# A decoder layer on one core: six of eight pairs of gate tiles computed with seven block products instead of eight

## The chip, the core and the metric

The kernel runs on one core of a Trainium2 chip. The metric is the time of one execution in device microseconds. Engines are named as the profile names them: PE is TensorE (PEld its weight loads), DVE is VectorE, ACT is ScalarE, POOL is GpSimd, SP is SyncE, which here only issues DMAs. Each engine works through its own list of instructions in the order in which the program gave them, and a semaphore holds it where it needs another engine's result.

## The reference, cut to what matters

One layer of a decoder for 512 prompt tokens and 64 sample tokens (576 in all), model width 1024. Around the change it computes

```python
z = jnp.einsum('btd,dn->btn', x, w_in)                     # conv B, C, h | q, k, v | two gates of 1024 columns
...
gates = jax.nn.sigmoid(z[..., -2 * D_MODEL:] + b_gate)
mixed = gates[..., :D_MODEL] * (yc @ w_conv_out) + gates[..., D_MODEL:] * (ya @ w_attn_out)
x1 = layer_norm(ALPHA * x + mixed @ w_o, ln1_g, ln1_b)
hid = jnp.square(jax.nn.relu(x1 @ w_up))
x2 = layer_norm(ALPHA * x1 + hid @ w_down, ln2_g, ln2_b)
```

with `yc` the output of a short convolution and `ya` that of attention over three head groups. All of it is float32.

## The kernel before, in words

**Products.** Every float32 operand of a large product is split into a rounded part (hi, an fp32r copy made by ACT) and the rest (lo, source minus hi, made by DVE). A product is then three passes on PE: hi by hi, hi by lo, lo by hi (`PASSES`). Activations stand transposed, features on the 128 partitions, and the 576 tokens are two blocks of 288 columns, so that one matmul is a 128x128 weight against 128x288.

**Weights.** All weights are cut into 126 units of 128x1024 (four bytes each, 512 KB). A `Stream` loads them by SP into a ring of four buffers (`raw`), and splits them into a ring of five (`hl`). `get(u)` gives unit u and writes the splits of the next ones into the lists of ACT and DVE at that place. The order of all work is written out by hand: what the Python code emits first stands first in an engine's list.

**Stages.** Queries and keys; values; the convolution with attention's softmax and values put between; then the gates, which the change touches; the output projection `o` (line 1028); the first norm; and the feed-forward part in four quarters, up (`up_pair`) and down.

**The gates (lines 953 to 981).** For each j of 8 there are two gate tiles (units u and u+1, 48 matmuls each, named `zg`), and one unit of 768 columns that holds `w_conv_out` and `w_attn_out` for the same 128 features (36 matmuls, named `zm`: 24 for the convolution, 12 for attention). ACT makes the sigmoids from PSUM (line 964), DVE multiplies the two `zm` tiles by them (line 973) and adds (976), and ACT and DVE split the sum into `mxhl` (lines 542 and 543), which the output projection reads. A `zg` or `zm` tile takes two PSUM banks and there are two such tiles; of the other four banks two are used as `s` and two as `ya0` and `ya1` in the stages before, and lie idle in the gates.

**Seven products (`up_pair`, line 1166).** The up part of the feed-forward uses already what the change brings to the gates. Two weight tiles A and B of 1024 inputs against two blocks of tokens are a product of 2 by 2 blocks (A1, A2 and B1, B2 are the halves over the inputs): eight block products of 12 matmuls each. A Strassen-Winograd scheme does it with seven, of sums of weight blocks and sums of x blocks. The weights come as four pieces: `hu` (unit A as it is), `hs` and `hc` (two tiles of sums), and `hd` (half of unit B). `raws` holds the sums: SP loads B2 and A1 into it, POOL issues a DMA that adds B1 to both (`accum_op`, line 327), and DVE adds A1 and A2 later (lines 367 and 369). The sums of x are made by DVE, and split as everything is. PE then makes seven products into three banks (`a`, `Y`, `X`). After the first product ACT copies bank `a` away (`p1`, line 1178), the third product adds on in `a`, and DVE makes the outputs from `Y`, `X` and `p1` (lines 1183 to 1204). `Stream.queue`, `load`, `hi`, `lo`, `pump` and `next` (lines 293 to 392) keep that: `hi` writes the next ACT cast of a weight piece if its ring has a free buffer, `lo` the next DVE job behind it.

Of the kernel before, what the change touches and what calls it, by code (L numbers as in the profile page):

```python
# [20 lines left out]
F32 = mybir.dt.float32  # L21
# [219 lines left out]
class Stream:  # L241


    def __init__(self, nc, pool, wall):
        self.nc, self.pool, self.wall = nc, pool, wall
        self.raw, self.hl = {}, {}
        self.loaded = self.done = 2
        self.last = FIRST_F + ALONE - 1
# [41 lines left out]
        return self.hl.pop(u)  # L290


    def queue(self, items, pool, held):
# [15 lines left out]
        self.got = {}

        self.hls.held = [[t, False] for t in held]

    def load(self):
        Q = self.nc.sync
        while self.loads:
            n, it = self.loads[0]
            rings = (self.raws,) if it[0] == "unit" else (self.raws, self.raws2, self.raw1)
            if not all(r.free() for r in rings):
                return
            self.loads.pop(0)  # L320
            one = self.wall[it[1] - 2]
            if it[0] == "pair":
                two = self.wall[it[2] - 2]
                sums = self.raws2.take(f"raws{it[1]}")
                Q.dma_start(sums[:, 0, :], two[:, 512:])
                Q.dma_start(sums[:, 1, :], one[:, :512])
                self.nc.gpsimd.dma_start(sums, two[:, :512].unsqueeze(1).broadcast_to((128, 2, 512)), accum_op=ALU.add)  # L327
            r = self.raws.take(f"raw{it[1]}")
            Q.dma_start(r, one)
            self.got[n] = [r]  # L330
            if it[0] == "pair":
                last = self.raw1.take(f"rawl{it[1]}")
                Q.dma_start(last, two[:, 512:])
                self.got[n] += [sums, last]

    def hi(self):

        self.load()
        if not self.pieces:
            return  # L340
        n, kind, ring = self.pieces[0]
        ring = getattr(self, ring)
        if n not in self.got or ring is None or not ring.free() or (kind == 2 and ("sum", n) in self.after):
# [6 lines left out]
        w = 512 if kind == 3 else 1024  # L350
        t = ring.take(f"h{'uscd'[kind]}{n}")
        self.nc.scalar.copy(t[:, 0, :w], src[:, :w])  # L352
# [81 lines left out]
def _decoder_step(ctx, tc, nc, a):  # L434
# [86 lines left out]
    def last_rows(pool, x, name):  # L521

        t = pool.tile([128, 8, 2, 64], F32R, tag=name, name=name)
        for s in range(2):
            G.tensor_copy(t[:, :, s, :], x[:, s, :, 512:576])
        return t.rearrange("p k s n -> p k (s n)")

    def rows_of(x, last, xs, k, t):
        return x[:, xs, k, 128 * t:128 * t + 128] if t < 4 else last[:, k, :]
# [421 lines left out]


    mx_stack, mxpool = pool("mx", "right")
    mxhl = mxpool.tile([128, 2, 8, NT], F32R, tag="mxhl", name="mxhl")
    gt_stack, gtpool = pool("gt")
    for j in range(8):
        sg = []
        for i in range(2):
            z, zs = z_tile(f"zg{j}{i}")
            f_tile(stream.get(u), xhl, 8, zs)  # L960
            u += 1
            t = gtpool.tile([128, 2, NB], F32, tag=f"sg{i}", name=f"sg{j}{i}")
            c = C_BG + 8 * i + j
            S.activation(t, z, AF.Sigmoid, bias=con[:, c:c + 1], scale=1.0)  # L964
            sg.append(t)
        w = stream.get(u)
        u += 1
        m = []
        for i, (x, nk, w0) in enumerate(((ychl, 4, 0), (yahl, 2, 512))):
            z, zs = z_tile(f"zm{j}{i}")  # L970
            f_tile(w, x, nk, zs, w0)
            t = gtpool.tile([128, 2, NB], F32, tag=f"m{i}", name=f"m{j}{i}")
            V.tensor_tensor(t, z, sg[i], ALU.mult)  # L973
            m.append(t)
        mm = gtpool.tile([128, 2, NB], F32, tag="mm", name=f"mm{j}")
        V.tensor_tensor(mm, m[0], m[1], ALU.add)
# [96 lines left out]
    for i in range(4):  # L1073
        b_tile(f"none{i}")
    outs = [b_tile(f"o0{t}") for t in range(5)]
    for kk in range(4):
        w = stream.get(u)
        u += 1
# [4 lines left out]
    ws = [stream.get(u + kk, 7 - kk) for kk in range(4)]  # L1083
    u += 4
    for t in range(5):
        out = b_tile(f"o1{t}")
        for kk in range(4):
# [63 lines left out]
        return (lambda: S.copy(x1T[:, 0, m], t),  # L1151
                lambda: V.tensor_tensor(x1T[:, 1, m], t, x1T[:, 0, m].bitcast(F32), ALU.subtract))

    def product(z, w, w0, x, start):
        for i in range(4):
            for n, (ws, xs) in enumerate(PASSES):
                T.matmul(z, lhsT=w[:, ws, w0 + 128 * i:w0 + 128 * i + 128], rhs=x(xs, i),  # L1157
                         start=(start and i == 0 and n == 0), stop=(i == 3 and n == 2), skip_group_check=True)
# [7 lines left out]
    def up_pair(q, f, prev):  # L1166

        h = stream.next()
        ha, hb, hc, hd = (h[kind] for kind in range(4))
        z, Y, X = (half_bank(f"{b}{q}{f}") for b in "aYX")  # L1170
        p1 = fp.tile([128, NB], F32, tag="p1", name=f"p1{q}{f}", bufs=2)
        cc = cc_tile(f"cc{q}{f}")
        product(z, ha, 0, part_of(0, 0), True)
        stream.hi()
        prev[0]()
        stream.lo()
        product(Y, hc, 0, sum_of(2), True)
        S.copy(p1, z)
        prev[1]()
        stream.lo()  # L1180
        product(z, ha, 512, part_of(1, 0), False)
        stream.hls.done(ha)
        V.tensor_tensor(cc[:, 2], Y, p1, ALU.add)
        prev[2]()
        stream.lo()
        product(Y, hb, 0, sum_of(0), False)
        S.activation(cc[:, 0], z, AF.Relu)
        prev[3]()
        stream.hi()
        product(X, hb, 512, sum_of(1), True)  # L1190
        stream.hls.done(hb)
        V.tensor_tensor(cc[:, 3], Y, p1, ALU.add)
        stream.lo()
        stream.hi()
        product(Y, hc, 512, part_of(1, 1), False)
        stream.hls.done(hc)
        V.tensor_tensor(cc[:, 3], X, cc[:, 3], ALU.add)
        stream.lo()
        stream.hi()
        product(X, hd, 0, sum_of(3), False)  # L1200
        stream.hl1.done(hd)
        V.tensor_tensor(cc[:, 1], Y, p1, ALU.add)
        stream.lo()
        V.tensor_tensor(cc[:, 2], X, cc[:, 2], ALU.add)
# [206 lines left out]
```

## Time and profile before

| what | value |
|---|---|
| median of 3 runs | 852.58 us (852.41 to 853.11) |
| profiled execution, its own time | 852.76 us, span 850.7 us, clock 0.995 |
| gates, first `zg` to first `o` matmul | 247.51 to 389.32 us |
| one j of the gates | 17.60 us, of it 12.80 `zg` and 4.80 `zm` |
| busy in 250 to 300 us | PE 50.0, DVE 17.1, ACT 14.1, POOL 0 us |
| busy in 450 to 500 us (pairs of up, start of down) | PE 49.8, DVE 39.2, ACT 37.3, POOL 1.6 us |

How to read the views: a row of the timeline has the start, the length, the engine, the line, the operation, output and input tiles, the shape, how many instructions were put together, and in brackets how long the engine was idle before and what ended that. A row of the groups has busy time and mean nanoseconds of one, then the idle time before them. A matmul's length in the trace covers its way through the array, and matmuls overlap: what one costs in a stream is seen from the starts, not from the lengths.

### The profile page before, as it was taken

Reading aid. Unit: us, or ns where it says so; the run is one execution under the profiler, and the core shown is the slowest. Engines: PE = TensorE matmul, PEld = TensorE weight load, DVE = VectorE, ACT = ScalarE, POOL = GpSimd, SP = SyncE. Lnnn points to the kernel's source line nnn. Section 1 sums busy time; section 2 is a strip of 40 time slices with the busy share of each in tenths; the row PEclk is TensorE's granted clock in tenths of the full one; section 3 lists DMA queues with packets and bytes.
Section 4 is the critical chain, followed back from the end, with each engine's and each line's share of the span. In section 5 each row is a group of like instructions: output and inputs, shape, how many; then the busy total and the mean of one; then the engine's idle time right before and its main releaser. Section 6 shows DMA issues by size and latency. Waiting matters only on the chain.

```text
span 850.7 us, 14971 instructions
## 1 busy us (share of the span) xinstructions
PE 832.0 (98%) x6312; PEld 803.2 (94%) x6312; DVE 452.8 (53%) x747; ACT 317.0 (37%) x531; POOL 78.9 (9%) x117
## 2 busy tenths in 40 slices
PE   7999999999999999999999999999999999999994
PEld 7999999898889999998889999999999999999993
DVE  6545555574243344334769753476345753476465
ACT  6111126822223223322359631266114641266231
POOL 0212000137000000001001010000100000000013
PEclk9999999999999999999999999999999999999997
DMA  9687653871212232335207262444635262453111
GB/s 342 221 283 245 217 174 129 301 271 47 67 53 73 83 93 70 93 92 185 83 20 205 73 193 67 115 123 145 152 88 137 75 186 63 112 137 125 50 44 68
DMA packets 37762, 112.68 MB, mean 132 GB/s; under 512 B 4640, under 2 KB 4960, under 8 KB 37536
## 3 DMA queue, kind: packets, MB, share of 16 engines
q1 hardware_dynamic: 33840, 102.30, 36.7%
q0 software_dynamic: 3856, 9.44, 5.6%
q8 instruction: 49, 0.80, 0.4%
q14 instruction: 17, 0.14, 0.0%
HBM read 93.85 MB, written 16.42 MB: 130 GB/s over the span
## 4 chain that ended last, share of the span: by engine, by line
PE 94%; DVE 4%; ACT 1%; DMA 0%; issue 0%; POOL 0%; ACTq 0%
PE d L1126 18%; PE zg L512 12%; PE Y L1157 8%; PE d L1119 6%; PE o L1028 6%; PE a L1157 5%; PE X L1157 5%; PE v L879 5%; PE zA L512 5%; PE zm L512 5%; PE zB L512 4%; PE zh L512 3%; PE zc L512 2%; PE zb L512 2%; PE u L1119 2%; PE ya L720 1%
## 5 line engine op out<-in xcount | busy, mean ns | idle before, releaser
L1126 PE MATMUL d<-hid,hu 128*128 128x288 f32 x1152 | 154.1, 296 | 0.0
L1126 PEld LDWEIGHTS d<-hid,hu 128*128 128x128 f32 x1152 | 153.8, 189 | 0.0
L267 DVE TENSOR_TENSOR hl<-raw,hl 128x1024 fp32r<-128x1024 f32 (+1 forms) x64 | 76.4, 1204 | 102.3 <-ACT hl L266 102.0
L512 PE MATMUL zg<-xhl,hl 128*128 128x288 f32 x768 | 103.7, 296 | 0.0
L512 PEld LDWEIGHTS zg<-xhl,hl 128*128 128x128 f32 x768 | 102.8, 189 | 0.0
L266 ACT CAST hl<-raw 128x1024 fp32r<-128x1024 f32 (+1 forms) x64 | 65.0, 1020 | 67.3 <-PE zA L512 26.6
L352 ACT CAST hu<-raw 128x1024 fp32r<-128x1024 f32 x46 | 47.6, 1049 | 53.3 <-PE d L1126 37.7
L372 DVE TENSOR_TENSOR hu<-raw,hu 128x1024 fp32r<-128x1024 f32 x46 | 55.5, 1217 | 1.2 <-ACT hu L352 1.2
L1119 PE MATMUL d<-hid,hu 128*128 128x320 f32 (+1 forms) x384 | 53.4, 298 | 0.0
L1119 PEld LDWEIGHTS d<-hid,hu 128*128 128x128 f32 x384 | 51.5, 189 | 0.0
L1157 PE MATMUL a<-x1hl,hu 128*128 128x288 f32 x336 | 49.9, 297 | 0.0
L512 PE MATMUL zA<-xhl,hl 128*128 128x288 f32 x288 | 43.1, 304 | 4.5 <-ACT xhl L490 4.5
L1157 PEld LDWEIGHTS a<-x1hl,hu 128*128 128x128 f32 x336 | 46.6, 188 | 0.3
L1028 PE MATMUL o<-hl,mxhl 128*128 128x512 f32 x192 | 45.6, 394 | 0.8 <-DVE m L973 0.8
L512 PEld LDWEIGHTS zA<-xhl,hl 128*128 128x128 f32 x288 | 40.4, 194 | 5.6 <-ACT xhl L490 4.5
L1028 PEld LDWEIGHTS o<-hl,mxhl 128*128 128x128 f32 x192 | 35.8, 188 | 9.0 <-DVE m L973 1.1
L327 POOL DMA_DIRECT2D raws<-in_wall x14 | 16.9, 1207 | 281.2 <-DMA raws<-in_wall 152.5
L1356 DVE TENSOR_TENSOR yT<-yT,d 128x288 f32<-128x288 f32 x32 | 13.1, 451 | 51.7 <-PE d L1126 51.7
L879 PE MATMUL v<-hl,xhl 128*128 128x256 f32 x288 | 37.7, 287 | 0.0
L879 PEld LDWEIGHTS v<-hl,xhl 128*128 128x128 f32 x288 | 35.3, 191 | 2.1 <-issue 1.6
L964 ACT ACTIVATE sg<-zg,con 128x576 f32<-128x576 f32 x16 | 11.9, 741 | 59.2 <-PE zg L512 59.2
L512 PE MATMUL zB<-xhl,hl 128*128 128x288 f32 x240 | 33.5, 297 | 0.0
(202 smaller groups left out, 1308.6 us busy)
## 6 DMA issues: line engine op xcount, KB each, us to landing
raw<-in_wall SPq DMA_DIRECT2D x102, 512.0 KB, 4.7
raws<-in_wall SPq DMA_DIRECT2D x28, 256.0 KB, 4.2
raws<-in_wall POOLq DMA_DIRECT2D x14, 512.0 KB, 8.5
kc<-in_kc SPq DMA_DIRECT2D x8, 512.0 KB, 4.2
out_kc_out<-kc SPq DMA_DIRECT2D x8, 512.0 KB, 6.4
vc<-in_vc SPq DMA_DIRECT2D x8, 512.0 KB, 5.6
out_vc_out<-vc SPq DMA_DIRECT2D x8, 512.0 KB, 8.3
rawl<-in_wall SPq DMA_DIRECT2D x14, 256.0 KB, 4.3
```

What stands on the lines that cost most here:

```text
L266: self.nc.scalar.copy(hl[:, 0, :w], raw[:, :w])
L267: self.nc.vector.tensor_tensor(hl[:, 1, :w], raw[:, :w], hl[:, 0, :w].bitcast(F32), ALU.subtract)
L327: self.nc.gpsimd.dma_start(sums, two[:, :512].unsqueeze(1).broadcast_to((128, 2, 512)), accum_op=ALU.add)
L352: self.nc.scalar.copy(t[:, 0, :w], src[:, :w])
L372: V.tensor_tensor(t[:, 1, :w], src[:, :w], t[:, 0, :w].bitcast(F32), ALU.subtract)
L512: T.matmul(z[blk], lhsT=w[:, ws, w0 + 128 * k:w0 + 128 * k + 128], rhs=x[:, xs, k, NB * blk:NB * blk + NB], start=(k == 0 and n == 0), sto ...
L879: T.matmul(out, lhsT=rows_of(xhl, xlast, xs, k, t), rhs=wk[:, ws, kk:kk + 256], start=(k == 0 and n == 0), stop=(k == 7 and n == len(passe ...
L1028: T.matmul(out, lhsT=rows_of(mxhl, mlast, xs, k, t), rhs=w[:, ws, 512 * i:512 * i + 512], start=(k == 0 and m == 0), stop=(k == 7 and m == ...
L1119: T.matmul(z, lhsT=w[:, ws, 128 * k:128 * k + 128], rhs=x[:, xs, k, FB[blk]], start=(k == 0 and n == 0), stop=(k == 7 and n == 2), skip_gr ...
L1126: T.matmul(z[blk], lhsT=w[:, ws, 128 * k:128 * k + 128], rhs=x[:, xs, k, NB * blk:NB * blk + NB], start=(k == 0 and n == 0), stop=(k == 7 ...
L1157: T.matmul(z, lhsT=w[:, ws, w0 + 128 * i:w0 + 128 * i + 128], rhs=x(xs, i), start=(start and i == 0 and n == 0), stop=(i == 3 and n == 2), ...
L1356: V.tensor_tensor(y, y, z[blk], ALU.add)
```

## The change: what it does

For j = 2 to 7 the two gate tiles are a pair of seven products; j = 0 and 1 stay as they were. The body of `up_pair` becomes a function `pair`, used by the gates and by `up_pair`. In the gates its three banks are the idle `s`, `ya0` and `ya1`.

- `xr`: x is loaded once more, as float32, in two DMAs of 1.15 MB, into the place where the second half of `mxhl` will be. `gate_sum` makes the four sums of its blocks in place (DVE, line 1017 and on, then a cast by ACT, line 1024), `gate_low` the rest (DVE, line 1027). Sums 0 and 1 stand behind the merge of j = 0, sums 2 and 3 behind the two gate tiles of j = 1.
- The units 36 to 58 (six pairs, their `zm` units, and five units of the output projection) come by `queue` rather than by `get`. The sums of a pair are now a load of their own. The order of pieces in the gates is hs, hd, hc, hu.
- `merge` does what lines 968 to 977 did; the sigmoids lie in one tile `cc`, with one buffer, and the products and the sum are written into it.
- `mxhl` becomes two tiles, `mxa` and `mxb`, for j = 0 to 3 and 4 to 7.

```diff
+    def gate_sum(m):
...
+        if m == 0:
+            V.tensor_tensor(b11, b11, b12, ALU.subtract)
...
+        S.copy(xT[:, 0, m], (b11, b12, b22, b21)[m])
+    def gate_low(m):
+        V.tensor_tensor(xT[:, 1, m], (b11, b12, b22, b21)[m], xT[:, 0, m].bitcast(F32), ALU.subtract)
...
     for j in range(8):
-            S.activation(t, z, AF.Sigmoid, bias=con[:, c:c + 1], scale=1.0)
...
-        split_into(mxhl[:, 0, j], mxhl[:, 1, j], flat(mm))
+        cc = gtpool.tile([128, 4, NB], F32, tag="cc", name=f"gc{j}")
+        if j < G_ALONE:
...
+                if j == 0 and i == 0:
+                    Q.dma_start(xr[:, 0:4, :], a["start"][:, 0:4, 256:])
+                    Q.dma_start(xr[:, 4:8, :], a["start"][:, 4:8, 256:])
+                    stream.queue(items, gtpool, [], (1, 3, 2, 0))
...
+                f_tile(w, xhl, 8, zs)
+                u += 1
+                if j:
+                    stream.hls.done(w)
+                    gate_sum((2, 3)[i])
+                S.activation(cc[:, 2 * i:2 * i + 2], z, AF.Sigmoid, bias=bias(i, j), scale=1.0)
+                if j:
+                    gate_low((2, 3)[i])
+                    stream.pump(2)
+            w = stream.get(u)
+            merge(j, w, cc)
...
+        else:
+            p1 = gtpool.tile([128, NB], F32, tag="p1", name=f"gp{j}", bufs=2)
...
+            pair(stream.next(), [t[:, :NB] for t in banks], p1, cc,
...
+            S.activation(cc[:, 1], cc[:, 1], AF.Sigmoid, bias=bias(0, j), scale=1.0)
+            S.activation(cc[:, 2:4], cc[:, 2:4], AF.Sigmoid, bias=bias(1, j), scale=-1.0)
+            w, = stream.next().values()
+            merge(j, w, cc)
+            stream.hls.done(w)
+            stream.pump()
```

The start of `pair`, as it now serves both stages:

```python
        product(z, ha, 0, part_of(0, 0), True)      # product 1 into bank a
        stream.hi()
        prev[0]()
        stream.lo()
        product(Y, hc, 0, sum_of(2), True)          # product 2 into Y
        S.copy(p1, z)
        prev[1]()
        stream.lo()
        product(z, ha, 512, part_of(1, 0), False)   # product 3, adds on in a
        stream.hls.done(ha)
        V.tensor_tensor(cc[:, 2], Y, p1, ALU.add)
        prev[2]()
        stream.lo()
        product(Y, hb, 0, sum_of(0), False)         # product 4, adds on in Y
```

**Where the instructions stand now, first place: ACT between the merge of one j and the next.** Before (ACT, from the merge of j = 1 to the merge of j = 2; `hl39` and on are the splits of weight units, `sg` the sigmoids):

```order
L542 CAST mxhl_2786<-mm1_3112 128x576
L266 CAST hl39_3117<-raw39_2957 128x1024
L964 ACTIVATE sg20_3170<-zg20_3116,con_63 128x576
L266 CAST hl40_3173<-raw40_3013 128x1024
L964 ACTIVATE sg21_3226<-zg21_3172,con_63 128x576
L266 CAST hl41_3228<-raw41_3068 128x768
L542 CAST mxhl_2786<-mm2_3275 128x576
```

With the change (ACT, from the merge of j = 2 to the merge of j = 3; `gp3` is `p1` and `ga3` bank `a` of pair 3, `hs4`, `hd4`, `hc4` and `hu4` the pieces of the pair after, `hu5` the 768 columns of that pair's `zm` unit):

```order
L595 CAST mxa_2792<-gc2_3155 128x576
L359 CAST hs4_3321<-raws42_3138 128x1024
L359 CAST hd4_3341<-rawl42_3144 128x512
L559 COPY gp3_3325<-ga3_3326 128x288
L1092 ACTIVATE gc3_3324<-ga3_3326,con_63 128x288
L359 CAST hc4_3398<-raws42_3138 128x1024
L359 CAST hu4_3418<-raw42_3142 128x1024
L1093 ACTIVATE gc3_3324<-gc3_3324,con_63 128x288
L1094 ACTIVATE gc3_3324<-gc3_3324,con_63 128x576
L359 CAST hu5_3466<-raw44_3153 128x768
L595 CAST mxa_2792<-gc3_3324 128x576
```

The copy of bank `a` stands behind the merge's cast of the j before and behind two casts of weight pieces; before there was nothing between the merge's cast and the next sigmoid but one weight cast.

**Second place: DVE from the merge of j = 0 to the first pair** (`hs0`, `hu0`, `hd0`, `hc0` are the pieces of the pair j = 2):

```order
L596 TENSOR_TENSOR mxa_2792<-gc0_2795,mxa_2792 128x576
L1017 TENSOR_TENSOR xr_2793<-xr_2793 128x4x288
L1019 TENSOR_TENSOR xr_2793<-xr_2793 128x4x288
L1027 TENSOR_TENSOR xT_2794<-xr_2793,xT_2794 128x1152 x2
L1021 SCALAR_TENSOR_TENSOR xr_2793<-xr_2793 128x4x288
L1027 TENSOR_TENSOR xT_2794<-xr_2793,xT_2794 128x1152
L379 TENSOR_TENSOR hs0_3030<-raws36_2802,hs0_3030 128x1024
L374 TENSOR_TENSOR raws36_2802<-raws36_2802,raw36_2962 128x512
L1023 SCALAR_TENSOR_TENSOR xr_2793<-xr_2793 128x4x288
L1027 TENSOR_TENSOR xT_2794<-xr_2793,xT_2794 128x1152
L376 TENSOR_TENSOR raws36_2802<-raws36_2802,raw36_2962 128x512
L379 TENSOR_TENSOR hu0_3033<-raw36_2962,hu0_3033 128x1024
```

Behind them come the rest of `hd0`, the product with `zm10`, the rest of `hc0`, and the product with `zm11`. Before, three splits of weight units stood in their place. ACT's list there reads: three casts of sums, the sigmoid of `zg10`, casts of `hs0` and `hu0`, the cast of the fourth sum, the sigmoid of `zg11`, casts of `hd0`, `hc0`, `hu1`, the merge's cast, `hs2`, `hd2`, the copy of bank `a`.

**Third place: DVE behind the merge of j = 2:**

```order
L596 TENSOR_TENSOR mxa_2792<-gc2_3155,mxa_2792 128x576
L379 TENSOR_TENSOR hs4_3321<-raws42_3138,hs4_3321 128x1024
L374 TENSOR_TENSOR raws42_3138<-raws42_3138,raw42_3142 128x512
L376 TENSOR_TENSOR raws42_3138<-raws42_3138,raw42_3142 128x512
L564 TENSOR_TENSOR gc3_3324<-gY3_3327,gp3_3325 128x288
```

The first reading of bank `Y` (line 564) stands behind the merge's split, the split of `hs4` and both sums of weights for the pair after; before, one split of a weight unit stood behind the merge. Pair 7 has only one split of a unit (`hu12`) in the place of the three.

More of the change, by code (lines that the diff above doesn't have):

```diff
@@ L315, in load @@
         while self.loads:
-            n, it = self.loads[0]
-            rings = (self.raws,) if it[0] == "unit" else (self.raws, self.raws2, self.raw1)
-            if not all(r.free() for r in rings):
+            n, it, sums = self.loads[0]
+            rings = (self.raws2,) if sums else (self.raws,) if it[0] == "unit" else (self.raws, self.raw1)
+            if not all(r.free() for r in rings) or (self.sums_only and not sums):
                 return
@@ L342, in hi @@
         ring = getattr(self, ring)
-        if n not in self.got or ring is None or not ring.free() or (kind == 2 and ("sum", n) in self.after):
+        if n not in self.got or self.got[n][0] is None or ring is None or not ring.free() or (kind == 2 and ("sum", n) in self.after):
             return
@@ L523, in last_rows, with product, pair @@
         t = pool.tile([128, 8, 2, 64], F32R, tag=name, name=name)
[L524 to L525 removed]
+        n = 8 // len(x)
+        for i, part in enumerate(x):
+            for s in range(2):
+                G.tensor_copy(t[:, n * i:n * i + n, s, :], part[:, s, :, 512:576])
         return t.rearrange("p k s n -> p k (s n)")
     def rows_of(x, last, xs, k, t):
[L529 removed]
+        n = 8 // len(x)
+        return x[k // n][:, xs, k % n, 128 * t:128 * t + 128] if t < 4 else last[:, k, :]
     def passes_of(t):
         return PASSES if t < 4 else ((0, 0), (0, 1))
+    def product(z, w, w0, x, start):
+        for i in range(4):
+            for n, (ws, xs) in enumerate(PASSES):
+                T.matmul(z, lhsT=w[:, ws, w0 + 128 * i:w0 + 128 * i + 128], rhs=x(xs, i),
+                         start=(start and i == 0 and n == 0), stop=(i == 3 and n == 2), skip_group_check=True)
+    def pair(h, banks, p1, cc, part_of, sum_of, prev, eleven):
+        ha, hb, hc, hd = (h[kind] for kind in range(4))
+        z, Y, X = banks
+        product(z, ha, 0, part_of(0, 0), True)
+        stream.hi()
+        prev[0]()
+        stream.lo()
+        product(Y, hc, 0, sum_of(2), True)
+        S.copy(p1, z)
+        prev[1]()
+        stream.lo()
+        product(z, ha, 512, part_of(1, 0), False)
+        stream.hls.done(ha)
+        V.tensor_tensor(cc[:, 2], Y, p1, ALU.add)
+        prev[2]()
+        stream.lo()
+        product(Y, hb, 0, sum_of(0), False)
+        eleven(cc[:, 0], z)
+        prev[3]()
+        stream.hi()
+        product(X, hb, 512, sum_of(1), True)
+        stream.hls.done(hb)
+        V.tensor_tensor(cc[:, 3], Y, p1, ALU.add)
+        stream.lo()
+        stream.hi()
+        product(Y, hc, 512, part_of(1, 1), False)
+        stream.hls.done(hc)
+        V.tensor_tensor(cc[:, 3], X, cc[:, 3], ALU.add)
+        stream.lo()
+        stream.hi()
+        product(X, hd, 0, sum_of(3), False)
+        stream.hl1.done(hd)
+        V.tensor_tensor(cc[:, 1], Y, p1, ALU.add)
+        stream.lo()
+        V.tensor_tensor(cc[:, 2], X, cc[:, 2], ALU.add)
     def z_tile(name):
@@ L1075, in _decoder_step @@
     outs = [b_tile(f"o0{t}") for t in range(5)]
+    stream.last = FIRST_F + ALONE - 1
+    stream.loaded = stream.done = FIRST_O + 5
     for kk in range(4):
-        w = stream.get(u)
-        u += 1
+        w, = stream.next().values()
         for t in range(5):
@@ L1082, in _decoder_step @@
                 o_add(outs[t], t, 0)
-    ws = [stream.get(u + kk, 7 - kk) for kk in range(4)]
-    u += 4
+        if kk == 0:
+            assert not stream.after or len(stream.pieces) == 0
+        while stream.pieces or stream.after:
+            stream.pump()
+            if kk < 2:
+                break
+        if not stream.pieces and not stream.after and kk < 3:
+            stream.prepare(FIRST_O + 5 + kk, 0)
+    ws = list(stream.next().values()) + [stream.get(FIRST_O + 5 + kk, 6 - kk) for kk in range(3)]
+    u = FIRST_F
     for t in range(5):
@@ L1168, in up_pair @@
         h = stream.next()
-        ha, hb, hc, hd = (h[kind] for kind in range(4))
-        z, Y, X = (half_bank(f"{b}{q}{f}") for b in "aYX")
+        cc = cc_tile(f"cc{q}{f}")
         p1 = fp.tile([128, NB], F32, tag="p1", name=f"p1{q}{f}", bufs=2)
[L1172 to L1204, printed above, removed]
+        pair(h, [half_bank(f"{b}{q}{f}") for b in "aYX"], p1, cc, part_of, sum_of, prev,
+             lambda c, z: S.activation(c, z, AF.Relu))
         def rectify():
```

117 lines of the change are left out of this document (77 added, 40 removed).

## The prediction

> **What bounds the kernel now.** I read the page first, then the timeline of the gates engine by engine, then the groups of instructions for prices, then the pairs of the feed-forward part, where the same scheme runs already.
>
> ```profile
> span 850.7 us, 14971 instructions
> PE 832.0 (98%) x6312; PEld 803.2 (94%) x6312; DVE 452.8 (53%) x747; ACT 317.0 (37%) x531; POOL 78.9 (9%) x117
> PE 94%; DVE 4%; ACT 1%; DMA 0%; issue 0%; POOL 0%; ACTq 0%
> ```
>
> PE is busy for 98% of the span and holds 94% of the chain that ended last. So a matmul less is time less, if PE still never waits. In the gates it does not wait at all (PE, one j):
>
> ```profile
> 282.71 12.96 PE L512 MATMUL zg<-xhl,hl 128*128 128x288 f32 x96
> 295.51 3.36 PE L512 MATMUL zm<-ychl,hl 128*128 128x288 f32 x24
> 298.71 1.76 PE L512 MATMUL zm<-yahl,hl 128*128 128x288 f32 x12
> 300.31 12.96 PE L512 MATMUL zg<-xhl,hl 128*128 128x288 f32 x96
> ```
>
> One j takes 300.31 - 282.71 = 17.60 us for 132 matmuls, 0.1333 us each; 12 of them, a product, take 1.60.
>
> **What is removed.** Six pairs times 12 matmuls: 72 x 0.1333 = 9.60 us. An undisturbed pair with its `zm` would take 16.00. Added: on PE nothing; on ACT and DVE casts, sums and copies. Over a whole j both have room (they are busy 14.1 and 17.1 of 50 us in a stretch of the gates, by the table above). But the order written by hand decides, since PE waits for single instructions in those lists: product 3 for the copy of bank `a`, product 4 for DVE's first reading of `Y`. So I follow both lists from row to row.
>
> **A pair in the middle (j = 3 to 6).** Let t0 be the end of the `zm` before it, where the pair's first product starts. What the merge does after t0 is in the trace, since 282.71 is such a moment (DVE, then ACT, then how the last merge lets go of PE):
>
> ```profile
> 282.91 0.76 DVE L973 TENSOR_TENSOR m<-zm,sg 128x576 f32<-128x576 f32 x1 [0.84 <-PE zm L512]
> 283.70 0.76 DVE L976 TENSOR_TENSOR mm<-m,m 128x576 f32<-128x576 f32 x1
> 285.20 0.76 DVE L543 TENSOR_TENSOR mxhl<-mm,mxhl 128x576 fp32r<-128x576 f32 x1 [0.74 <-ACT mxhl L542]
> 286.15 1.23 DVE L267 TENSOR_TENSOR hl<-raw,hl 128x1024 fp32r<-128x1024 f32 x1 [0.20 <-ACT hl L266]
> ...
> 284.49 0.67 ACT L542 CAST mxhl<-mm 128x576 fp32r<-128x576 f32 x1 [4.86 <-DVE mm L976]
> 285.07 1.05 ACT L266 CAST hl<-raw 128x1024 fp32r<-128x1024 f32 x1
> ...
> 388.51 0.76 DVE L973 TENSOR_TENSOR m<-zm,sg 128x576 f32<-128x576 f32 x1 [0.84 <-PE zm L512]
> ```
>
> ACT's cast for the merge starts at t0 + 1.78 and the cast behind it at t0 + 2.36, 0.09 before the first ends. DVE's next split starts at t0 + 3.44. The new work has its prices in the feed-forward part (groups, with mean ns):
>
> ```profile
> L352 ACT CAST hs<-raws 128x1024 fp32r<-128x1024 f32 x14 | 14.7, 1050 | 37.3 <-PE d L1126 32.1 <-PE X L1157 5.2
> L352 ACT CAST hd<-rawl 128x512 fp32r<-128x512 f32 x14 | 8.6, 618 | 0.0
> L1178 ACT COPY p<-a 128x288 f32<-128x288 f32 x14 | 5.6, 398 | 4.8 <-PE a L1157 4.8
> L372 DVE TENSOR_TENSOR hs<-raws,hs 128x1024 fp32r<-128x1024 f32 x14 | 17.1, 1220 | 2.5 <-ACT hs L352 2.5
> L367 DVE TENSOR_TENSOR raws<-raws,raw 128x512 f32<-128x512 f32 x14 | 9.6, 689 | 0.3
> L1183 DVE TENSOR_TENSOR cc<-Y,p 128x288 f32<-128x288 f32 x14 | 6.4, 456 | 14.6 <-PE Y L1157 14.6
> L1152 DVE TENSOR_TENSOR x1T<-xs,x1T 128x1152 fp32r<-128x1152 f32 x4 | 5.4, 1352 | 0.2 <-ACT x1T L1151 0.2
> L1151 ACT CAST x1T<-xs 128x1152 fp32r<-128x1152 f32 x4 | 4.6, 1152 | 1.4 <-DVE xs L1149 1.4
> ```
>
> *ACT:* `hs` for the next pair from t0 + 2.36, handed over 0.09 before its end: + 0.96; `hd` + 0.53; the copy of `a` from t0 + 3.85 to 4.25. PE goes on 0.05 after a release (the merge's last product ends at 388.51 + 0.76 = 389.27, PE starts at 389.32 below): 4.30. Product 3 would start at t0 + 3.20: **1.10 late**. *DVE:* the split of `hs` from t0 + 3.44, 1.22; two sums of weights, 2 x 0.69; the first reading of `Y`, 0.46: t0 + 6.50, and PE 0.05 later. Product 4 would start at t0 + 4.80: **1.75 late in all** (the 1.10 lie within). The rest of the pair fits: product 7 ends at t0 + 12.95, and all that stands behind on DVE (about 4 us of splits and readings) ends with it. So a middle pair takes 17.75, its own saving of 1.60 and 0.15 more; four of them cost 4 x 1.75 = **7.00**.
>
> In the feed-forward part the same code has no such wait:
>
> ```profile
> 482.64 1.83 PE L1157 MATMUL a<-x1hl,hu 128*128 128x288 f32 x12
> 484.32 1.76 PE L1157 MATMUL Y<-x1T,hc 128*128 128x288 f32 x12
> 485.92 1.76 PE L1157 MATMUL a<-x1hl,hu 128*128 128x288 f32 x12
> 487.52 1.76 PE L1157 MATMUL Y<-x1T,hs 128*128 128x288 f32 x12
> ...
> 484.52 0.40 ACT L1178 COPY p<-a 128x288 f32<-128x288 f32 x1 [0.49 <-PE a L1157]
> ```
>
> There ACT waits for bank `a` (0.49 idle) and copies at once; no merge's cast, which cannot begin before t0 + 1.78, stands ahead of it.
>
> **The last pair (j = 7)** has only one cast ahead of the copy: 2.36 + 0.96 + 0.40 + 0.05 = t0 + 3.77, **0.57** late; DVE is done by 3.44 + 1.22 + 0.46 = 5.12, before product 3 ends at 5.37.
>
> **The first pair (j = 2).** The list of DVE behind the merge of j = 0 is longer than a j. That merge's split starts one j before 285.20, at 267.60, and I let the list go on from 268.3. Sums 0 and 1 (1.36 each, taken as the 1.35 of the splits of their size) end at 271.0, their splits (1.27 each with the handover) at 273.6, sum 2 at 274.9. Its cast on ACT ends at 276.1, its split at 277.5. ACT goes on with a sigmoid, `hs0` and `hu0` to 278.65; DVE splits `hs0` to 278.95, a sum of weights to 279.65, sum 3 to 280.95. Its cast on ACT ends at 282.15; the sigmoid of `zg11` stands behind it and ends at 282.8. The last tile of `zm` needs the banks of `zg11`: it starts at 282.85 instead of 298.71 - 17.60 = 281.11, **1.75 late**. DVE: split of sum 3 to 283.5, a sum 284.2, `hu0` 285.35. Product 1 started at 284.45 and needs that for its third matmul: **0.65**. Then `hd0` 285.95, the product with `zm10` 286.65, `hc0` 287.8; product 2 needs it at 287.0: **0.85**. The product with `zm11` and the addition end at 289.25, then ACT: the merge's cast, `hs2`, `hd2`, the copy, 291.8; product 3 would have started at 289.2: **2.65**. DVE reads `Y` by 293.95 instead of 293.45: **0.55**. Sum **6.45**.
>
> **What a wait costs beside itself.** The first products of `o` come after a wait:
>
> ```profile
> 389.32 5.73 PE L1028 MATMUL o<-hl,mxhl 128*128 128x512 f32 x24 [0.85 <-DVE m L973]
> 395.07 1.20 PE L1028 MATMUL o<-hl,mlast 128*128 128x512 f32 x4
> 396.11 5.63 PE L1028 MATMUL o<-hl,mxhl 128*128 128x512 f32 x24
> 401.58 1.09 PE L1028 MATMUL o<-hl,mlast 128*128 128x512 f32 x4
> ```
>
> 24 matmuls took 5.75 there and 5.47 later: 0.28 for starting again. A wait that a later wait swallows costs none, so six count (the last of each pair). Between 0 and 0.28 I take 0.20: **1.20**.
>
> **The transfers.** x once more, the sums and the pieces lie beside PE:
>
> ```profile
> 239.28 0.34 SPq L947 DMA_DIRECT2D out_ust<-ust  x1
> ...
> 249.21 0.76 DVE L543 TENSOR_TENSOR ychl<-yf,ychl 128x576 fp32r<-128x576 f32 x1 [0.74 <-ACT ychl L542]
> ...
> R<-in_xr SPq DMA_DIRECT2D x1, 2048.0 KB, 9.1
> raws<-in_wall SPq DMA_DIRECT2D x28, 256.0 KB, 4.2
> raws<-in_wall POOLq DMA_DIRECT2D x14, 512.0 KB, 8.5
> ```
>
> SP issues `xr` behind `ust`, near 240; 2.36 MB at the rate of `R` (2048 KB in 9.1) land near 251, 17 us before sum 0. SP then stands until the convolution's tiles are free, near 250; the sums of the first pair have landed (4.2 for the loads, 8.5 for POOL's addition) near 264, needed at 276.7. The sums for pair 4 can be loaded when `hc0` is split (287.8) and land near 302; ACT wants them near 307. So POOL's queue holds nobody up by these rows, with 5 us to spare at its tightest place. Behind the gates nothing changes: `R` and the units behind it wait for the end of the merge as before.
>
> **Sum.** -9.60 + 6.45 + 7.00 + 0.57 + 1.20 = +5.62 us. Against the profiled execution, 852.76 (span 850.7 and 2.06 around it), that is 858.4; the median of the runs, 852.58, lies 0.18 below, so I predict **858.2**. *Bounds.* First pair: DVE without any wait for ACT has 17.3 us of work from 268.3 to `hc0`, so product 2 is 1.0 late at least, and the wait for the copy stays: 4.2; above, with a slower clock (below), 8. Middle pairs: 1.10 each if DVE's reading came in time, 2.20 if both waits added to more: 4.4 to 8.8. Starts: 0 to 1.7. From 852.58 - 0.6 = 852.0 to about 862.
>
> **Rivals.** *The middle pairs run without waits:* then -9.60 + 6.45 + 0.6 for one start again = -2.55, **850.0**, faster. It decides at the copy: if it ends by t0 + 3.2. For it: ACT is busy 28% of the time. Against it: the merge's cast cannot start before t0 + 1.78, and two casts of 1.49 together stand between. 9%. *All of it is hidden*, 852.58 - 9.6 = **843.0**: it needs the first pair's list of 17.3 us in 14.4 as well; 2%. *PE's clock falls in the first pair:* the program's first matmuls, after an idle start, were slow:
>
> ```profile
> 4.48 1.95 PE L512 MATMUL zA<-xhl,hl 128*128 128x288 f32 x6 [4.48 <-ACT xhl L490]
> 6.23 1.65 PE L512 MATMUL zB_first<-xhl,hl 128*128 128x288 f32 x6
> 7.67 1.56 PE L512 MATMUL zA<-xhl,hl 128*128 128x288 f32 x6
> 9.06 0.96 PE L512 MATMUL zB_first<-xhl,hl 128*128 128x288 f32 x6
> ```
>
> 18 matmuls took 9.06 - 4.48 = 4.58 instead of 2.40. If a wait in the gates did that once, 2.2 more: **860.4**. The longest wait that I work out is 2.65, against the 4.48 here; 10%. [...] *POOL's additions come late:* the sums of a pair land after ACT reaches `hs`, and ACT stands with the copy behind it. At 5 us of slack they would have to take 13.5 instead of 8.5; then each us more is one more in a pair, some 3 in all: **861**. 7%.
>
> **How the numbers follow.** Forecast 72%; the rivals 9, 2, 10 and 7. A measurement of this kernel tells about 0.2% (1.7 us) from no change: faster is below 850.9, slower above 854.3. Faster: most of the first rival and the second, 10%. Same: its remainder and the low end of the bounds, 9%. Slower: 81%. The range is that of the bounds, 852.0 to 862.0; outside lie the two fast rivals and a part of the last, under 20%.
>
> **What would show it.** Right: gaps on PE in front of the third and fourth product of every pair, released by ACT's copy and by DVE's reading of `Y`, a j of 17.7 to 18.0 us for j = 3 to 6, and 24 or so from the start of the last `zm` tile of j = 1 to the start of j = 3. Wrong: a j near 16.0; a gap ended by a DMA; a gap behind the gates; a granted clock under 1 in the first pair.

## The result: 0.8% slower, and the profile after

The changed kernel takes 859.29 us (median of 4 runs, 858.85 to 860.0) against 852.85 of the kernel before beside it: a ratio of 1.0077, 95% interval 1.0059 to 1.0094. The forecast was 858.2, slower. The profiled execution took 860.0, with a span of 858.1.

From the page of the changed kernel, the engines and the chain that ended last (its shares by engine):

```profile
PE 827.7 (96%) x6240; PEld 795.7 (93%) x6240; DVE 493.0 (57%) x809; ACT 334.7 (39%) x559; POOL 85.2 (10%) x125
PE 84%; DVE 10%; ACT 3%; issue 2%; DMA 1%; POOL 0%; ACTq 0%; DVEq 0%
```

PE has its 72 matmuls less, but its share of the chain fell from 94% to 84%; DVE took 10% instead of 4%. Where they stand in PE's way, the waits of PE between 248 and 396 us say (who waited, for whom, us in all, times, longest):

```profile
PE ga L547 <- ACT gp L559: 6.8, 6, 2.3
PE gY L547 <- DVE gc L564: 1.7, 4, 0.4
```

Six waits for the copy of bank `a` (line 559), one a pair; four for DVE's first reading of `Y` (line 564), one in each middle pair. One of 1.50 for a sigmoid in front of the first pair, and two short ones for splits behind it, stand in the timeline below. No DMA is among them. PE's timeline from the `zm` tiles of j = 1 to the last one of the gates:

```profile
278.56 3.36 PE L519 MATMUL zm<-ychl,hl 128*128 128x288 f32 x24
283.42 1.85 PE L519 MATMUL zm<-yahl,hl 128*128 128x288 f32 x12 [1.50 <-ACT gc L1070]
285.11 0.42 PE L547 MATMUL ga<-xhl,hu 128*128 128x288 f32 x2
285.91 1.59 PE L547 MATMUL ga<-xhl,hu 128*128 128x288 f32 x10 [0.38 <-DVE hu L379]
287.34 0.42 PE L547 MATMUL gY<-xT,hc 128*128 128x288 f32 x2
288.31 1.59 PE L547 MATMUL gY<-xT,hc 128*128 128x288 f32 x10 [0.56 <-DVE hc L379]
292.24 2.14 PE L547 MATMUL ga<-xhl,hu 128*128 128x288 f32 x12 [2.33 <-ACT gp L559]
294.37 3.04 PE L547 MATMUL gY<-xT,hs 128*128 128x288 f32 x12
...
302.04 3.35 PE L519 MATMUL zm<-ychl,hu 128*128 128x288 f32 x24
...
306.83 1.74 PE L547 MATMUL ga<-xhl,hu 128*128 128x288 f32 x12
...
311.16 1.85 PE L547 MATMUL ga<-xhl,hu 128*128 128x288 f32 x12 [1.00 <-ACT gp L559]
313.43 1.86 PE L547 MATMUL gY<-xT,hs 128*128 128x288 f32 x12 [0.41 <-DVE gc L564]
...
324.72 1.74 PE L547 MATMUL ga<-xhl,hu 128*128 128x288 f32 x12
...
378.38 1.74 PE L547 MATMUL ga<-xhl,hu 128*128 128x288 f32 x12
...
393.45 1.76 PE L519 MATMUL zm<-yahl,hu 128*128 128x288 f32 x12
```

A middle j takes 324.72 - 306.83 = 17.89 us, more than the 17.60 of the kernel before although it has 12 matmuls less. The two lists that hold it, ACT's and then DVE's, for the pair of j = 3:

```profile
308.67 0.68 ACT L595 CAST mxa<-gc 128x576 fp32r<-128x576 f32 x1 [4.44 <-DVE gc L1040]
309.25 1.04 ACT L359 CAST hs<-raws 128x1024 fp32r<-128x1024 f32 x1
310.20 0.62 ACT L359 CAST hd<-rawl 128x512 fp32r<-128x512 f32 x1
310.72 0.39 ACT L559 COPY gp<-ga 128x288 f32<-128x288 f32 x1
...
310.33 1.22 DVE L379 TENSOR_TENSOR hs<-raws,hs 128x1024 fp32r<-128x1024 f32 x1 [0.19 <-ACT hs L359]
311.59 0.69 DVE L374 TENSOR_TENSOR raws<-raws,raw 128x512 f32<-128x512 f32 x1
312.31 0.69 DVE L376 TENSOR_TENSOR raws<-raws,raw 128x512 f32<-128x512 f32 x1
312.92 0.45 DVE L564 TENSOR_TENSOR gc<-gY,gp 128x288 f32<-128x288 f32 x1
```

Product 1 had ended 1.60 behind its start, near 308.4. ACT copied its bank at 310.72, behind three casts, and PE started 0.05 behind the copy's end. DVE read `Y` from 312.92, behind the split of `hs` and two sums, and PE started again 0.06 behind that. The pieces cast and split there belong to the next pair, so nothing needs them yet.

The forecast's working can be set beside this: product 3 started 4.33 behind the pair's start where it had 4.30, and product 4 6.60 where it had 6.55.

In the first pair something else shows. The fourth product was slow with no wait shown in front of it (294.37 to 297.25, where a product takes 1.60), and the windows have the reason (columns: window, its length, busy time of PE, PEld, DVE, ACT and POOL with counts, granted clock, DMA share, GB/s):

```profile
292.00:294.00 2.00, 1.76 (x12) 1.77 (x12) 1.97 (x4) 0.18 (x1) 1.04 (x1) 0.90 0.83 316
294.00:296.00 2.00, 2.00 (x9) 1.66 (x9) 0.91 (x2) 1.55 (x2) 0.16 (x1) 0.50 0.77 230
296.00:298.00 2.00, 2.00 (x13) 2.00 (x13) 0.56 (x2) 0.00 (x0) 0.00 (x0) 0.75 1.12 202
298.00:300.00 2.00, 2.00 (x17) 2.00 (x16) 1.46 (x3) 0.96 (x1) 0.00 (x0) 1.00 0.14 22
```

The granted clock fell to a half behind the 2.33 us wait: 9 matmuls fall in a window of 2 us where 17 are usual.

### The profile page after: what moved, and what is told of

It reads as the page before. It is cut to its first block, busy times and chain, and to the rows that moved or that the text cites. A ratio compares the mean times of both kernels' runs of the same rounds, so it can differ in the third digit from the quotient of the medians.

```text
span 858.1 us, 15003 instructions
## 1 busy us (share of the span) xinstructions
PE 827.7 (96%) x6240; PEld 795.7 (93%) x6240; DVE 493.0 (57%) x809; ACT 334.7 (39%) x559; POOL 85.2 (10%) x125
## 4 chain that ended last, share of the span: by engine, by line
PE 84%; DVE 10%; ACT 3%; issue 2%; DMA 1%; POOL 0%; ACTq 0%; DVEq 0%
PE d L1259 18%; PE Y L547 8%; PE d L1252 6%; PE a L547 5%; PE X L547 5%; PE v L932 5%; PE zA L519 5%; PE zB L519 4%; PE o L1152 4%; PE zm L519 3%; PE zh L519 3%; PE zc L519 2%; PE zb L519 2%; PE u L1252 2%; PE gY L547 2%; PE gX L547 2%
## 5 line engine op out<-in xcount | busy, mean ns | idle before, releaser
L359 ACT CAST hu<-raw 128x1024 fp32r<-128x1024 f32 (+1 forms) x63 | 64.0, 1027 | 67.9 <-PE d L1259 32.4
L379 DVE TENSOR_TENSOR hu<-raw,hu 128x1024 fp32r<-128x1024 f32 (+1 forms) x63 | 74.8, 1195 | 11.2 <-ACT hu L359 11.2
L269 DVE TENSOR_TENSOR hl<-raw,hl 128x1024 fp32r<-128x1024 f32 (+1 forms) x41 | 48.9, 1209 | 42.2 <-ACT hl L268 42.0
L268 ACT CAST hl<-raw 128x1024 fp32r<-128x1024 f32 (+1 forms) x41 | 42.3, 1039 | 68.7 <-PE zB L519 23.5
L331 POOL DMA_DIRECT2D raws<-in_wall x20 | 24.2, 1209 | 375.2 <-DMA raws<-in_wall 275.6
L359 ACT CAST hc<-raws 128x1024 fp32r<-128x1024 f32 x20 | 20.9, 1044 | 41.3 <-DVE raws L376 41.3
L359 ACT CAST hs<-raws 128x1024 fp32r<-128x1024 f32 x20 | 21.0, 1048 | 37.3 <-PE d L1259 32.1
L519 PEld LDWEIGHTS zB<-xhl,hl 128*128 128x128 f32 x240 | 32.3, 189 | 0.9 <-issue 0.6
L519 PE MATMUL zh<-xhl,hl 128*128 128x288 f32 x192 | 29.9, 303 | 0.0
L519 PE MATMUL zc<-xhl,hl 128*128 128x288 f32 x192 | 29.1, 301 | 0.0
```

The costliest lines, as they stand in the source:

```text
L268: self.nc.scalar.copy(hl[:, 0, :w], raw[:, :w])
L269: self.nc.vector.tensor_tensor(hl[:, 1, :w], raw[:, :w], hl[:, 0, :w].bitcast(F32), ALU.subtract)
L331: self.nc.gpsimd.dma_start(t, two[:, :512].unsqueeze(1).broadcast_to((128, 2, 512)), accum_op=ALU.add)
L379: V.tensor_tensor(t[:, 1, :w], src[:, :w], t[:, 0, :w].bitcast(F32), ALU.subtract)
L519: T.matmul(z[blk], lhsT=w[:, ws, w0 + 128 * k:w0 + 128 * k + 128], rhs=x[:, xs, k, NB * blk:NB * blk + NB], start=(k == 0 and n == 0), sto ...
```

## The experiments

All alter the changed kernel, and are timed beside the kernel before (852.74 to 852.78 us). The lists are altered in the pairs of the gates alone; the pairs of the feed-forward part keep the old order by a switch, which the diffs leave out, as they do the `prev` calls, empty in the gates. The first three test whether ACT's list and DVE's each hold PE in a pair.

**Copy ahead of the casts.**

```diff
             product(z, ha, 0, part_of(0, 0), True)
+            S.copy(p1, z)
+            stream.pump()
             stream.hi()
             stream.lo()
             product(Y, hc, 0, sum_of(2), True)
-            S.copy(p1, z)
...
             stream.hls.done(w)
-            stream.pump()
+            if j == 7:
+                stream.pump()
```

The pump that stood behind the merge, and writes the cast and the split of `hs`, moves behind the copy; DVE's order stays.

> The change with one list altered: in the pairs of the gates ACT's copy of bank a stands directly behind the merge's cast, ahead of the casts of hs and hd; DVE's list is as in the change. Theory (each of the two lists holds PE by itself): product 3 starts on time (the copy ends about t0 + 2.85, t0 being the end of the zm before), but hs is cast later (2.85 to 3.9), its split by DVE and the two sums behind it later too (to 6.4), and the first reading of Y ends near 6.9, so product 4 is 2.15 late instead of 4.8: a middle j of 18.1 to 18.2 us instead of 17.89, no gain. All together 859 to 861 us, against 859.3 for the change. Rival (ACT's copy is the only real wait, and DVE's reading comes late just because all before it came late): a middle j of 16.0 to 16.4, about 853 us.

Measured: 863.63 us, ratio 1.0128 (1.0113 to 1.0143). PE's timeline at three pairs:

```profile
306.27 1.74 PE L547 MATMUL ga<-xhl,hu 128*128 128x288 f32 x12
...
313.16 1.86 PE L547 MATMUL gY<-xT,hs 128*128 128x288 f32 x12 [1.98 <-DVE gc L564]
...
324.45 1.74 PE L547 MATMUL ga<-xhl,hu 128*128 128x288 f32 x12
...
331.34 2.67 PE L547 MATMUL gY<-xT,hs 128*128 128x288 f32 x12 [1.98 <-DVE gc L564]
...
344.15 1.74 PE L547 MATMUL ga<-xhl,hu 128*128 128x288 f32 x12
```

The wait for the copy is gone in the middle pairs, and the wait for the reading of `Y` has grown from 0.41 to 1.98: a middle j of 324.45 - 306.27 = 18.18. So DVE's list is a wait of its own, which the rival had denied. The expected range ended at 861. What lies above it is in two of the four middle pairs, which took 19.70 (344.15 - 324.45) and 19.69, 1.5 longer than the other two, with the same wait of 1.98: there the clock fell (0.57 over 332 to 336 us and over 352 to 356; windows' columns as above).

```profile
332.00:336.00 4.00, 4.00 (x21) 4.00 (x20) 0.46 (x1) 0.00 (x0) 0.00 (x0) 0.57 0.01 4
```

**Reading ahead of the splits.**

```diff
+            stream.hi()
             product(z, ha, 0, part_of(0, 0), True)
             stream.hi()
-            stream.lo()
             product(Y, hc, 0, sum_of(2), True)
             S.copy(p1, z)
-            stream.lo()
...
             V.tensor_tensor(cc[:, 2], Y, p1, ALU.add)
+            stream.lo()
+            stream.lo()
+            stream.lo()
             stream.lo()
```

The pump behind the merge is gone, and its cast is the `hi` ahead of product 1. The splits of `hs` and `hd` and the two sums of weights, three of which stood ahead of the reading, are written behind it; ACT's order stays.

> The change with the other list altered: DVE's first reading of Y stands directly behind the merge's split, ahead of the split of hs and the sums of weights; ACT's list is as in the change. Theory: product 3 still waits for the copy, 1.0 to 1.1 late; the reading follows the copy at once (t0 + 4.75) and is done before product 3 ends (5.9), so product 4 waits for nothing: a middle j of 17.0 to 17.2 us; the first pair 0.5 shorter. 859.3 - 4 x 0.8 - 0.5 = 855.6 us. Rival (DVE's reading is not what holds product 4, but only stands beside something else): a middle j of 17.8 to 17.9 and 859 us.

Measured: 856.34 us, ratio 1.0043 (1.0028 to 1.0058). The middle pairs:

```profile
306.03 1.74 PE L547 MATMUL ga<-xhl,hu 128*128 128x288 f32 x12
310.36 1.85 PE L547 MATMUL ga<-xhl,hu 128*128 128x288 f32 x12 [1.00 <-ACT gp L559]
...
323.23 1.74 PE L547 MATMUL ga<-xhl,hu 128*128 128x288 f32 x12
```

A j of 323.23 - 306.03 = 17.20 with the copy's wait alone. The first pair gained only 0.25 (306.03 - 284.56 = 21.47 from its product 1 to the next pair's, where the change has 306.83 - 285.11 = 21.72), and the clock fell there as before (0.89, 0.50 and 0.76 in the windows of 2 us from 290).

**Both.** The copy and the reading stand first, the casts, splits and sums of the next pair's pieces behind them (the pump behind the merge is gone here too).

```diff
             product(z, ha, 0, part_of(0, 0), True)
-            stream.hi()
-            stream.lo()
             product(Y, hc, 0, sum_of(2), True)
             S.copy(p1, z)
-            stream.lo()
             product(z, ha, 512, part_of(1, 0), False)
             stream.hls.done(ha)
             V.tensor_tensor(cc[:, 2], Y, p1, ALU.add)
+            stream.pump()
+            stream.hi()
+            stream.lo()
+            stream.lo()
             stream.lo()
```

> Both lists altered: copy ahead of the casts, reading ahead of the splits and sums. Theory: no wait is left in the middle pairs and the last, a j of 16.0 us (84 matmuls and 36 of zm by 0.1333), four times 1.89 and 0.67 less; in the first pair the copy ends near 290.8 instead of 292.2, 1.4 less, and the wait in front of product 3 is near 1 us instead of 2.3, so the granted clock stays at 1.00 and another 1.3 comes back: 859.3 - 7.6 - 0.7 - 2.7 to 3.4 = 847 to 849 us, faster than before. Rival (the moved work comes back as a wait somewhere else in the pair, for a split of hs, hc or hu that is now late): a middle j over 16.4 with a gap in front of another product, 850 us or more. If the clock's fall hangs on the sum of several waits and not on the longest, it still falls: 1.3 more.

Measured: 848.01 us, ratio 0.9948 (0.9931 to 0.9965): faster than the kernel before. Product 3 of the first pair, and the starts of two middle pairs:

```profile
289.61 1.85 PE L547 MATMUL ga<-xhl,hu 128*128 128x288 f32 x12 [0.87 <-ACT gp L557]
...
302.61 1.74 PE L547 MATMUL ga<-xhl,hu 128*128 128x288 f32 x12
...
318.55 1.74 PE L547 MATMUL ga<-xhl,hu 128*128 128x288 f32 x12
```

A middle j is now 318.55 - 302.61 = 15.94, without a wait. The moved work found room elsewhere in the pair. In the first pair the three waits ahead of the copy's are as in the change, the copy's is 0.87 instead of 2.33, and the clock stayed at 1.00 (windows from 280 to 302 us).

**The sums of x in j = 0.** In this run each sum stands with its split, two behind each gate tile of j = 0, ahead of that tile's sigmoid; the lists in the pairs are the change's, and the old places of the sums are gone.

```diff
+                if not j:
+                    gate_sum(2 * i)
+                    gate_low(2 * i)
+                    gate_sum(2 * i + 1)
+                    gate_low(2 * i + 1)
                 S.activation(cc[:, 2 * i:2 * i + 2], z, AF.Sigmoid, bias=bias(i, j), scale=1.0)
```

> The lists in the pairs as in the change, but all four sums of x with their splits are made during j = 0 (sums 0 and 1 behind the first gate tile's list, 2 and 3 behind the second's) instead of behind the merge of j = 0 and in j = 1. Theory (the first pair's loss beyond a middle pair's is the list of sums): no wait for zg11's sigmoid, hu0 or hc0, the first pair loses 1.9 like a middle pair instead of 7.5, and the clock stays 1.00: 859.3 - 5.6 = 853.7 us. Rival (x arrives too late, or the sums in j = 0 hold up the splits of the weight units or the sigmoids there): gaps on PE between 247 and 283, 856 us or more.

Measured: 861.66 us, ratio 1.0108 (1.0093 to 1.0123). The rival's side, for a reason that ACT's list shows (PE's row stands below it):

```profile
267.78 1.15 ACT L1024 CAST xT<-xr 128x1152 fp32r<-128x1152 f32 x1 [2.69 <-DVE xr L1023]
...
269.63 3.25 PE L519 MATMUL zm<-yahl,hl 128*128 128x288 f32 x12 [5.38 <-ACT gc L1074]
```

A sum on DVE, its cast on ACT and its split on DVE, one behind the other, leave each engine waiting for the other: ACT 2.69 in the row above, and DVE then 1.22 for that cast. The sigmoid of the second tile came at 268.84, and PE had to wait 5.38 us for it in front of the second `zm` tile; the clock fell in that wait (0.56, 0.50, 0.50 and 0.73 in the windows of 2 us from 266, so at half from about 266.2 to 273.1). But the first pair behind it took 17.88 (290.45 to 308.33), like a middle pair. So the experiment was right on the first pair and had made a new wait of its own.

**The same, with the sums together.**

```diff
+                if not j and not i:
+                    for m in range(4):
+                        gate_sum(m)
+                    for m in range(4):
+                        gate_low(m)
```

> As the run with the sums of x made during j = 0, but mended: the four sums stand together behind the first gate tile, then their four splits, so that DVE and ACT do not wait for one another and the second tile's sigmoid is not held up. Lists in the pairs as in the change. Theory: no wait in front of zm11, hu0 and hc0, no fall of the clock; the first pair loses 1.9 like a middle pair. 859.3 - 5.6 = 853.7 us. Rival (the list of sums costs PE as much in j = 0 as it did in j = 1): a wait between 258 and 270 us, 856 us or more.

Measured: 854.34 us (10 runs), ratio 1.0017 (1.0008 to 1.0027). The starts of the first two pairs:

```profile
282.54 1.74 PE L547 MATMUL ga<-xhl,hu 128*128 128x288 f32 x12
...
300.43 1.74 PE L547 MATMUL ga<-xhl,hu 128*128 128x288 f32 x12
```

PE has no wait between 247 and 282 us, the first pair takes 300.43 - 282.54 = 17.89, and the mean granted clock of the profiled execution is 0.995, as in that of the kernel before, where the change has 0.993. The loss of the first pair beyond a middle one, and the clock's fall with it, was the place of the sums of x.

**All three places.** Both lists altered, and the sums of x together in j = 0.

> Both lists of the pairs altered (copy and reading of Y ahead) and the four sums of x made early in j = 0. Theory (the loss is those three places and nothing else): no wait on PE from 248 us to the end of the gates, a j of 15.9 to 16.0 for all six pairs; 852.7 - 9.6 and about 0.5 for the gap in the output projection that the change has and the kernel before has not: 843 to 844 us, the whole of the removed matmuls. Rival (PE gets other waits once these are gone, for sums of weights or transfers that were hidden by the lateness): 846 us or more, with a gap whose releaser is a DMA or a split of a weight piece.

Measured: 843.31 us, ratio 0.9887 (0.9873 to 0.9902). The only wait of PE from 248 to 396 us:

```profile
PE o L1163 <- DVE gc L1052: 0.9, 1, 0.9
```

That is the wait behind the last merge, which the kernel before has too. 852.78 - 843.31 = 9.47, of the 9.60 that the removed matmuls are worth. This is the version to keep.

**The gap in the output projection.** The changed kernel has a wait of 0.57 in front of the first transposes that the kernel before has not. Here two of the four unit splits ahead of it are moved.

```diff
-    ws = list(stream.next().values()) + [stream.get(FIRST_O + 5 + kk, 6 - kk) for kk in range(3)]
+    ws = list(stream.next().values()) + [stream.get(FIRST_O + 5 + kk, 4 - kk) for kk in range(3)]
...
         o_add(out, t, 1)
+        if t == 2:
+            stream.prepare(FIRST_O + 7, 4)
```

> As the run before (all three places mended), and in the output projection two of the four casts and splits of weight units that stand in one go ahead of the first norm are moved behind the third row block. Theory: the change's gap of 0.57 us in front of the first transposes (x1t) goes, since DVE gets to the additions to R two splits (2.3 us) earlier: 0.4 to 0.6 us less than the run before. Rival (the norm is late for another reason): the gap stays, or comes back behind the norm as a wait for the moved units.

Measured: 843.94 us, ratio 0.9895 (0.988 to 0.991), no gain over the run before. The transposes with a wait in that version and then in this one (its first ones, at 416.99, have none):

```profile
417.10 1.09 PE L1185 MATMUL x1t<-con,R 128*128 128x128 f32 x8 [0.57 <-ACT R L1157]
```

```profile
430.31 1.09 PE L1185 MATMUL x1t<-con,R 128*128 128x128 f32 x8 [0.23 <-ACT R L1157]
435.92 1.09 PE L1185 MATMUL x1t<-con,R 128*128 128x128 f32 x8 [0.83 <-ACT R L1157]
```

The gap was indeed the place of those two splits: it went when they moved, and 0.23 and 0.83 came back behind them. The rival's second half holds.

**How long may PE wait?** In the version with all three places mended, ACT makes the copy 6, 7, 9 and 11 times in the pairs of j = 3 to 6.

```diff
-            S.copy(p1, z)
+            for _ in range(1 + again):
+                S.copy(p1, z)
```

> All three places mended, and then the wait for bank a's copy put back in four sizes: in j = 3, 4, 5 and 6 ACT makes the copy 6, 7, 9 and 11 times instead of once, which should hold product 3 for about 1.5, 1.9, 2.6 and 3.3 us, with PE busy before and behind. Theory (the clock falls by what share of a few microseconds PE stands, as three falls behind waits of 1.75 to 2.34 us, and none in ten waits of 1.0 us, suggest): no fall at 1.5, perhaps one at 1.9, falls at 2.6 and 3.3, and a fall costs about 1.5 us beside the wait. [...]

Measured in one run: 859.02 us. Product 3 of the four pairs, the starts of the pairs that follow, and the clock around the second of the waits:

```profile
298.53 1.74 PE L547 MATMUL ga<-xhl,hu 128*128 128x288 f32 x12
303.55 1.86 PE L547 MATMUL ga<-xhl,hu 128*128 128x288 f32 x12 [1.69 <-ACT gp L558]
...
316.42 1.74 PE L547 MATMUL ga<-xhl,hu 128*128 128x288 f32 x12
321.86 2.67 PE L547 MATMUL ga<-xhl,hu 128*128 128x288 f32 x12 [2.11 <-ACT gp L558]
...
336.26 1.74 PE L547 MATMUL ga<-xhl,hu 128*128 128x288 f32 x12
342.56 2.85 PE L547 MATMUL ga<-xhl,hu 128*128 128x288 f32 x12 [2.97 <-ACT gp L558]
...
364.12 3.11 PE L547 MATMUL ga<-xhl,hu 128*128 128x288 f32 x12 [3.83 <-ACT gp L558]
```

```profile
322.00:326.00 4.00, 4.00 (x19) 4.00 (x20) 3.44 (x5) 2.27 (x4) 0.00 (x0) 0.57 0.00 0
```

Behind 1.69 the clock stayed (1.00 in all windows from 302 to 322 us); with 2.11, 2.97 and 3.83 it fell (0.57 over 4 us above, then 0.76, 0.50 and 0.88 in the windows of 2 us from 342, and 0.88, 0.50 and 0.76 in those from 362), as the theory forecast. The j of the first took 316.42 - 298.53 = 17.89, which is 15.94 + 1.69 + 0.26: so 0.26 is what this wait cost beside itself. The second took 19.84 = 15.94 + 2.11 + 0.26 + 1.53, with the same 0.26 taken, and 1.53 is the fall.

## Why the prediction was right, step by step

The forecast's reason holds: PE's saving is lost to two lists, written by hand, in which work for later stands ahead of the one instruction that PE waits for. The version that reorders both lists and moves the sums gives all of it back (843.31 us).

| term | forecast | measured in the profiled execution |
|---|---|---|
| `zm11` behind the sigmoid | 1.75 | 283.42 - 278.56 - 3.20 = 1.66 |
| split of `hu0` | 0.65 | 285.91 - 285.11 - 0.27 = 0.53 |
| split of `hc0` | 0.85 | 288.31 - 287.34 - 0.27 = 0.70 |
| copy in the first pair | 2.65 | 292.24 - 288.31 - 1.33 = 2.60 |
| rest of the first pair | 0.55 and a start | 302.04 - 292.24 - 8.00 = 1.80 |
| four middle pairs | 7.00 and 0.80 for starts | 378.38 - 306.83 - 64.00 = 7.55 |
| last pair | 0.57 and a start | 393.45 + 1.60 - 378.38 - 16.00 = 0.67 |

- **The middle pairs** came out at 17.89 where the text named 17.7 to 18.0, with the two waits at the two products, released as named. The copy's wait as a lone wait costs 17.20 - 15.94 = 1.26; the sum had 1.10 and a start.
- **The price of starting again** was 0.20 by choice. Measured as the sum counts it, a middle pair lost 17.89 - 16.00 = 1.89 where 1.75 was forecast without it, so 0.14. The 0.26 of the run with four sizes is counted otherwise, beyond the idle time that the trace shows.
- **The first pair** is where the sum was off. Its first four terms were forecast 0.05 to 0.15 too high. The fifth, DVE's reading, had 0.55 and a start, and moving the reading gained 0.25 there; the clock was left out. The clock's fall was a rival of its own with 10%, and it happened, beside the forecast and not instead of it. The step that failed is "The longest wait that I work out is 2.65, against the 4.48 here": a fall did not need a wait near 4.48, it came behind 2.33. Its size, 2.2, was taken from the start of the program; it cost 1.53 in the run above. Together with what was too high, the first pair and the `zm` tiles ahead of it took 306.83 - 278.56 = 28.27 where 20.80 is undisturbed: 7.47 against 6.65 (6.45 and a start).
- **"Behind the gates nothing changes"** failed by 0.57, the gap in front of the transposes. Four splits in one go ahead of the norm, where the kernel before has two, were not looked at.
- **The total** came within 1.09 (859.29 against 858.2), in part by luck. Left out were about 1.53 for the clock (the price in the run above) and 0.57 behind the gates. Against them three parts were forecast about 1.1 too high together: the first pair without its fall 6.65 against 5.94, the middle pairs 7.80 against 7.55, the last 0.77 against 0.67. A gap behind the gates and a clock under 1 in the first pair were two of the signs that the text had named for being wrong.
- **The start** of this profiled execution was 0.65 later at the first `zg` (248.16 against 247.51). It is not the change's: over the runs with the same program up to there that moment lay between 246.99 and 248.22.
- **The transfers** held nobody up: no wait of PE in the gates ends on a DMA, in any run. The rivals on POOL's additions, and the two fast ones, did not occur, though the version with all three mends shows that the second fast one (843.0) describes what this change is worth when its lists are in order.

## What to carry to other kernels

When a saving on the bound engine brings new single instructions that it waits for, write down each helper's list in the order of its emission and ask what stands ahead of that instruction; an engine that is busy for two fifths of the time (here ACT, 39%) can still be late by 1 us in every round (1.00 in a middle pair). Emit first what the bound engine waits for, then the work for the next round, and put work that is independent of everything (here the sums of x) where its engines idle, grouped so that two engines do not alternate. (The run that grouped the sums also took them out of the list ahead of the second tile's sigmoid; which of the two mattered was not tried apart.) A stage that worked elsewhere with the same code has no such guarantee once another step, here the merge, is put ahead of it.

## What the runs showed of the hardware

The granted clock of PE fell to a half behind waits much shorter than the 4.48 us that the prediction went by, and not behind each. Waits of 1.00 us with 0.41 behind them did not do it in the changed kernel (1.00 over 300 to 396 us), nor did its 1.50 (1.00 in the windows from 280 to 292), nor the 1.69 in the run with four sizes. Of the four middle waits of 1.98 in the run with the copy ahead, in the same place of the same loop, two did (0.57 over 4 us each) and two did not (a j of 18.18 and 18.17 instead of 19.70 and 19.69). With 2.11, 2.33, 2.34, 2.97, 3.83 and 5.38 it fell, and so it did with 1.75 that had 0.88 some 2.7 us before it (0.63 and 0.52 in the windows of 2 us from 294, in the run with the copy ahead).

The traces show how long a fall lasted: 0.57 over 4 us is 4 x 0.43 / 0.5 = 3.4 us at half clock, and the 0.90, 0.50 and 0.75 over 2 us each of the changed kernel give 3.4 again. With the wait of 5.38, the 0.56, 0.50, 0.50 and 0.73 over 2 us each make 6.8.

The length of a wait alone does not tell whether the clock falls, as the four of 1.98 show. What decides between them is not shown by these runs; the share of a few microseconds in the theory of the run with four sizes was the author's estimate.

The wait of 2.11 us cost 2.11 + 0.26 + 1.53 = 3.90 in all. A longer wait need not lose more at the clock: the one of 3.83 lost 1.27 (its j took 21.30 = 15.94 + 3.83 + 0.26 + 1.27), since the fall began near 363.5 (0.88 over 362 to 364 us), before PE went on at 364.12.
